# Key products with both token parts in one 512-column matmul, and an earlier first fetch of the gate grid

## The chip, the cores and the metric

One core of a Trainium2 chip runs the whole program. The metric is the device time of one execution in microseconds (us); lower is better. The engines are TensorE (PE; its weight loads are shown apart as PEld), VectorE (DVE), ScalarE (ACT), GpSimd (POOL) and SyncE (SP), whose queue issues nearly all of the transfers.

## The reference

Two transformer blocks over 256 tokens of width 1024, one after the other. Only the last part of the second matters here, a PEER layer: a retrieval among 128 x 128 = 16384 experts of one neuron each.

```
def peer(h, w_query, sub_keys, u_experts, v_experts):      # per chunk of 128 tokens
    qh = (xc @ w_query).reshape(128, 8, 256)
    s1, s2 = scores of the two halves of qh against 128 sub keys each
    v1, i1 = top_k(s1, 16);  v2, i2 = top_k(s2, 16)
    vs, ci = top_k(all 256 sums v1 + v2, 16)
    idx = e1 * 128 + e2                                    # the 16 experts of each head
    g = softmax(vs)
    z = einsum('td,thkd->thk', xc, u_experts[idx])         # key products
    a = gelu(z) * g
    return einsum('thk,thkd->td', a, v_experts[idx])       # value products
```

## The kernel before

Everything before the PEER layer is left alone by the change. The kernel computes the PEER layer densely: for all 16384 experts it forms the key products, and multiplies them by gates that are zero for the experts not chosen. Single precision is kept by splitting each operand into a rounded part `hi` and a rest `lo`, and summing three products, hi x hi, hi x lo and lo x hi (`mm3`, lines 118 to 122).

**Key stage.** 128 blocks of 128 experts (index `e2`) go through `up` (line 919). A block's weights (512 KB) are loaded by SP into a `raw` buffer (line 79, three buffers, loaded three blocks ahead), copied to `whi` by ScalarE (line 91) and subtracted to `wlo` by VectorE (line 92), two blocks ahead, three buffers each. Then 8 chunks of the depth, three matmuls each, 128 x 128 weights against 256 token columns, sum into one PSUM tile `pw` of the pool `psw` (two buffers): weights hi x tokens hi (line 120), hi x lo (line 121), lo x hi (line 122). ScalarE reads `pw` through the gelu into the tile `big` (line 928).

Beside these blocks the generator `select` (line 973) picks the experts of the 8 heads on VectorE, 1.25 steps for each block (`SEL_RATE`); every ninth block up to the 64th is preceded by two blocks of a head's query weights (`query`, line 954), which go through the same `mm3`. For each pair of heads it exponentiates on ScalarE (line 1030) and starts 32 indirect transfers on POOL (line 935), which add the gates of tokens 128 to 255 into a DRAM scratch `gscr`. When `select` is through, the gates of tokens 0 to 127 are made from one-hot matrices, 4 tokens at a time, in the remaining blocks: two one-hot tiles `o1` and `o2` on VectorE (line 1073, `GB` = 3 buffers each), a scaling on ScalarE (line 1076), four matmuls (line 1082), a multiplication into `big` for the blocks already there (line 1084, VectorE) and a copy for those to come (line 1086, ScalarE). A block that comes after some tokens' gates is then read in two parts: the tokens that are `done` through a small tile `gl` (lines 926, 927), the rest as before.

**Value stage.** For each pair of blocks, tokens 128 to 255 of `big` are multiplied by the gates fetched from `gscr` (`gated_pair`, lines 1122 and 1126; 256 KB fetched for each 4 blocks), `big` is split into `ah` and `al` (line 127), and for each block twelve matmuls of 512 columns (lines 356 to 358) add into four PSUM tiles `acc` of the pool `psa`. Its tiles lie in a pool `vs` that opens when the key stage's pool `gs` closes; `gf` and `fy` take the places of the token tiles `h2hi` and `h2lo`.

Instructions are put in an order on each engine by a planner that works with estimated durations; each engine then takes its own list strictly in that order. `issue_after(ins)` forces what is traced in the block behind `ins` on the same engine, without a wait.

Of the kernel before, what the change touches and what calls it, by code (L numbers as in the profile page):

```python
# [43 lines left out]
GB = 3  # L44
SB = 2
# [17 lines left out]
class Stream:  # L63
# [11 lines left out]
    def _load(self, i):  # L75
        ap = self.blocks[i]
        w = ap.shape[-1]
        r = self.pool.tile([P, self.width], F32, name="raw", tag="raw", bufs=self.raw_bufs)
        self.nc.sync.dma_start(out=r[:, :w], in_=ap)
        self.raw[i] = (r, w)  # L80

    def _split(self, i):
# [5 lines left out]
        with ExitStack() as es:  # L88
# [3 lines left out]
            self.nc.vector.tensor_sub(lo[:, :w], r[:, :w], hi[:, :w])  # L92
# [812 lines left out]
def peer(k, x, pool, hp, stream, u):  # L905
# [4 lines left out]
    with ExitStack() as es:  # L910
# [8 lines left out]
        def up(e2, done, gl):  # L919

            w = stream.next()
            ps = k.psw.tile([P, T], F32, name="pw", tag="w")
            end = wtype(k, w, 0, u, KC, ps)
            if done:
                g = gl.tile([P, P], F32, name="gl", tag="gl", bufs=2)
                nc.scalar.activation(g[:, :done], ps[:, :done], AF.Gelu_apprx_tanh)
                nc.vector.tensor_tensor(out=big[:, e2, :done], in0=g[:, :done], in1=big[:, e2, :done], op=ALU.mult)
            nc.scalar.activation(big[:, e2, done:], ps[:, done:], AF.Gelu_apprx_tanh)  # L928
# [17 lines left out]
        with k.tc.tile_pool(name="tk", bufs=1, reuse_waits="tile") as tk:  # L946
# [26 lines left out]
            def select():  # L973
                for h in range(H):
# [48 lines left out]
                    if h % 2:  # L1023
# [5 lines left out]
                                                op=ALU.subtract)  # L1029
                        nc.scalar.activation(e, e, AF.Exp)  # L1030
                        den = k.small.tile([P, 2, NT], F32, name="den", tag="den")
# [32 lines left out]
        with k.tc.tile_pool(name="gs", bufs=1, reuse_waits="tile") as gs:  # L1064
# [22 lines left out]

            done = made = 0
            start = e2
            ready = []  # L1090
            while e2 < P:
# [12 lines left out]
        with k.tc.tile_pool(name="vs", bufs=1, reuse_waits="tile") as gs:  # L1104
            gf = hp.tile([P, 2, D], F32, name="gf", tag="h2hi")
            ada_rows(k, gf[:, 0, :], 5)
            nc.sync.dma_start(out=gf[:, 1, :], in_=a["final_g"].to_broadcast([P, D]))
            fy = hp.tile([P, NT, D], F32, name="fy", tag="h2lo")
# [8 lines left out]
            grids = {}  # L1117

            def gated_pair(e0):
                if e0 % GQ == 0:  # L1120
                    g = grids[e0 // GQ] = gs.tile([P, GQ, P], F32, name="gt", tag="gt", bufs=2)
                    ins = nc.sync.dma_start(out=g, in_=grid[:, e0:e0 + GQ, :]).ins
                    for p in added:
                        k.tc.add_manual_dep(ins, p.name, order, reason="all heads have added their gates")
                b = big[:, e0:e0 + 2, P:]
                nc.vector.tensor_tensor(out=b, in0=b, in1=grids[e0 // GQ][:, e0 % GQ:e0 % GQ + 2, :], op=ALU.mult)  # L1126

            def parts(e0):
                ah = gs.tile([P, 2, T], F32R, name="ah", tag="ah", bufs=SB)
# [243 lines left out]
```

## Time and profile before

| | |
|---|---|
| three runs | 1714.48, 1718.57, 1720.56 us; median 1718.57 |
| profiled execution | 1715.93 us, its span 1714.2 us |
| mean granted TensorE clock | 0.991 of 2.4 GHz |
| busy over the span | PE 97%, PEld 89%, DVE 73%, ACT 50%, POOL 19% |
| key stage (from about 884 to 1342 us of the span) | 458 us |
| value stage (from about 1350 to 1702 us) | 352 us |

Busy time of an engine is the time in which at least one of its instructions runs. The span runs from the first to the last instruction; the execution is 1.7 us longer. A matmul's duration in the trace is longer than the time between two starts, because matmuls are pipelined; so rates are read from starts.

### The profile page before, as it was taken

Reading aid. Unit: us, or ns where it says so; the run is one execution under the profiler, and the core shown is the slowest. Engines: PE = TensorE matmul, PEld = TensorE weight load, DVE = VectorE, ACT = ScalarE, POOL = GpSimd, SP = SyncE. Lnnn points to the kernel's source line nnn. Section 1 sums busy time; section 2 is a strip of 40 time slices with the busy share of each in tenths; the row PEclk is TensorE's granted clock in tenths of the full one; section 3 lists DMA queues with packets and bytes.
Section 4 is the critical chain, followed back from the end, with each engine's and each line's share of the span. In section 5 each row is a group of like instructions: output and inputs, shape, how many; then the busy total and the mean of one; then the engine's idle time right before and its main releaser. Section 6 shows DMA issues by size and latency. Waiting matters only on the chain.

```text
span 1714.2 us, 28850 instructions
## 1 busy us (share of the span) xinstructions
PE 1670.0 (97%) x11106; PEld 1529.4 (89%) x11106; DVE 1252.1 (73%) x2081; ACT 864.2 (50%) x1399; POOL 318.5 (19%) x227
## 2 busy tenths in 40 slices
PE   8999999999999999999999999999999799999997
PEld 7899899888999999878889999999999688888886
DVE  6867789776867878865768878877777577555555
ACT  6554444336544544354544454457666344444443
POOL 1000000000000000036200787877700000000000
PEclk9999999999999999999999999999999899999999
DMA  8567678976456668966135777776655687666664
GB/s 312 181 196 217 202 248 289 360 237 208 136 160 185 225 183 294 339 215 205 60 118 182 176 186 172 173 173 149 156 153 160 209 281 238 193 195 187 195 188 131
DMA packets 115721, 345.70 MB, mean 202 GB/s; under 512 B 29856, under 2 KB 31104, under 8 KB 114688
## 3 DMA queue, kind: packets, MB, share of 16 engines
q1 hardware_dynamic: 95104, 336.23, 61.0%
q0 software_dynamic: 20480, 7.63, 4.2%
q8 instruction: 87, 1.43, 0.3%
q14 instruction: 50, 0.41, 0.1%
HBM read 342.66 MB, written 11.64 MB: 207 GB/s over the span
## 4 chain that ended last, share of the span: by engine, by line
PE 74%; issue 11%; DVE 8%; DMA 5%; ACT 2%; POOL 1%; SPq 0%; POOLq 0%; DVEq 0%; ACTq 0%
PE pw L122 13%; PE pw L121 13%; PE pw L120 13%; PE acc L358 10%; PE acc L357 10%; PE acc L356 10%; DMA gt<-gscr 3%; DVE wlo L92 2%; PE pst L1082 2%; PE po L476 1%; ACT whi L91 1%; PE pst L174 1%; DVE i L888 0%; PE pst L468 0%; DVE big L1126 0%
## 5 line engine op out<-in xcount | busy, mean ns | idle before, releaser
L91 ACT ACTIVATE whi<-raw 128x1024 fp32r<-128x1024 f32 (+1 forms) x549 | 573.3, 1048 | 593.6 <-PE pw L121 274.1
L92 DVE TENSOR_TENSOR wlo<-raw,whi 128x1024 fp32r<-128x1024 f32 (+1 forms) x549 | 667.2, 1220 | 252.3 <-ACT whi L91 246.2
L120 PE MATMUL pw<-h2hi,whi 128*128 128x256 f32 x1152 | 331.2, 287 | 0.9 <-ACT big L928 0.9
L122 PE MATMUL pw<-h2hi,wlo 128*128 128x256 f32 x1152 | 327.6, 284 | 1.8 <-DVE wlo L92 1.8
L121 PE MATMUL pw<-h2lo,whi 128*128 128x256 f32 x1152 | 327.3, 284 | 0.1
L120 PE MATMUL pw<-uhi,whi 128*128 128x256 f32 x1000 | 285.1, 285 | 0.0
L121 PE MATMUL pw<-ulo,whi 128*128 128x256 f32 x1000 | 284.4, 284 | 0.0
L122 PE MATMUL pw<-uhi,wlo 128*128 128x256 f32 x1000 | 284.4, 284 | 0.0
L935 POOL DMA_INDIRECT gscr<-gate,place x128 | 241.1, 1883 | 127.0 <-DVE first L1036 66.6
L122 PEld LDWEIGHTS pw<-h2hi,wlo 128*128 128x128 f32 x1152 | 222.2, 193 | 2.6 <-DVE wlo L92 2.6
L120 PEld LDWEIGHTS pw<-h2hi,whi 128*128 128x128 f32 x1152 | 222.4, 193 | 2.0 <-ACT big L928 1.7
L121 PEld LDWEIGHTS pw<-h2lo,whi 128*128 128x128 f32 x1152 | 222.4, 193 | 0.4 <-DVE h2lo L181 0.4
L356 PE MATMUL acc<-whi,ah 128*128 128x512 f32 x512 | 200.4, 391 | 8.1 <-ACT ah L127 8.1
L358 PE MATMUL acc<-whi,al 128*128 128x512 f32 x512 | 202.3, 395 | 0.4 <-DVE al L127 0.4
L357 PE MATMUL acc<-wlo,ah 128*128 128x512 f32 x512 | 201.4, 393 | 0.1
L121 PEld LDWEIGHTS pw<-ulo,whi 128*128 128x128 f32 x1000 | 192.5, 193 | 1.3 <-issue 1.3
L120 PEld LDWEIGHTS pw<-uhi,whi 128*128 128x128 f32 x1000 | 192.5, 192 | 0.9 <-issue 0.7
L122 PEld LDWEIGHTS pw<-uhi,wlo 128*128 128x128 f32 x1000 | 192.5, 193 | 0.7 <-issue 0.7
L356 PEld LDWEIGHTS acc<-whi,ah 128*128 128x128 f32 x512 | 96.7, 189 | 29.6 <-ACT ah L127 8.3
L357 PEld LDWEIGHTS acc<-wlo,ah 128*128 128x128 f32 x512 | 96.7, 189 | 23.0 <-DVE wlo L92 0.5
L358 PEld LDWEIGHTS acc<-whi,al 128*128 128x128 f32 x512 | 96.7, 189 | 20.9 <-DVE al L127 1.2
L356 PE MATMUL acc<-whi,hhi 128*128 128x512 f32 x256 | 99.9, 390 | 0.0
(257 smaller groups left out, 2411.0 us busy)
## 6 DMA issues: line engine op xcount, KB each, us to landing
raw<-in_w_layers_dram SPq DMA_DIRECT2D x240, 512.0 KB
raw<-in_u_dram SPq DMA_DIRECT2D x128, 512.0 KB
raw<-in_v_dram SPq DMA_DIRECT2D x128, 512.0 KB
aw<-in_w_ada_dram SPq DMA_DIRECT2D x48, 512.0 KB
gscr<-in_zeros_dram SPq DMA_DIRECT2D x16, 512.0 KB
raw<-in_w_query_dram SPq DMA_DIRECT2D x16, 512.0 KB
gt<-gscr SPq DMA_DIRECT2D x32, 256.0 KB
raw<-in_w_qkb_dram SPq DMA_DIRECT2D x8, 512.0 KB
```

The costliest lines, as they stand in the source:

```text
L91: self.nc.scalar.activation(hi[:, :w], r[:, :w], AF.Copy)
L92: self.nc.vector.tensor_sub(lo[:, :w], r[:, :w], hi[:, :w])
L120: nc.tensor.matmul(out, a[0], b[0], start=first, stop=False)
L121: nc.tensor.matmul(out, a[0], b[1], start=False, stop=False)
L122: return nc.tensor.matmul(out, a[1], b[0], start=False, stop=last).ins
L174: k.nc.tensor.transpose(ps[:, c, :], src[:, (c0 + c) * P:(c0 + c + 1) * P], k.ident)
L356: nc.tensor.matmul(acc, a[0], w[0][:, o:o + cols], start=first, stop=False)
L357: nc.tensor.matmul(acc, a[0], w[1][:, o:o + cols], start=False, stop=False)
L358: return nc.tensor.matmul(acc, a[1], w[0][:, o:o + cols], start=False, stop=last).ins
L476: nc.tensor.matmul(po[:, h, :], pT[:, i, :], v[:, c, vcol(h):vcol(h) + DH], start=(c == 0), stop=(c == nchunk - 1))
L935: ins = nc.gpsimd.indirect_dma_start(out=k.gscr, out_offset=bass.IndirectOffsetOnAxis(ap=place[:, h, j:j + 1], axis=0), in_=gate[:, h, j:j ...
L1082: nc.tensor.matmul(ps[:, i, :], o1[:, i, :], o2[:, i, :], start=True, stop=True)
```

## The change

It does four things. (1) The tokens' two parts lie beside each other in one tile `both`, and each chunk of a key block takes one matmul of 512 columns, weights hi x (tokens hi, tokens lo), and one of 256, weights lo x tokens hi. The two halves of the sum now lie in two halves of a PSUM tile of the pool `psa` (four buffers), and `total` joins them: ScalarE copies the second half, VectorE adds the first, ScalarE takes the gelu in place. Query blocks stay as they were. (2) The value stage's tiles share the key stage's pool, with `ah` and `al` in the places of `o1` and `o2` (two buffers each, one fewer than before), and its beginning moves into the key loop: the first fetch of the gates after the weight load issued last at block 120, the first two multiplications after the load and split issued last at block 125, and the first split before block 127. Each later fetch is issued one group of four blocks earlier. (3) `gf` and `fy` become parts of one tile in the place of `both`. (4) `select` pauses before and after its exponential, so that a pair of heads takes 23 steps instead of 21.

```
-GB = 3
-SB = 2
+GB = 2
+FETCH = 8
+AHEAD = 3
...
-        self.nc.sync.dma_start(out=r[:, :w], in_=ap)
+        self.last_load = self.nc.sync.dma_start(out=r[:, :w], in_=ap).ins
...
-            self.nc.vector.tensor_sub(lo[:, :w], r[:, :w], hi[:, :w])
+            self.last_split = self.nc.vector.tensor_sub(lo[:, :w], r[:, :w], hi[:, :w]).ins
...
-            ps = k.psw.tile([P, T], F32, name="pw", tag="w")
-            end = wtype(k, w, 0, u, KC, ps)
+            ps = k.psa.tile([P, 2, T], F32, name="pw", tag="acc")
+            for c in range(KC):
+                o = slice(c * P, (c + 1) * P)
+                nc.tensor.matmul(ps.rearrange("p i t -> p (i t)"), w[0][:, o], both[:, c].rearrange("p i t -> p (i t)"),
+                                 start=c == 0, stop=False)
+                end = nc.tensor.matmul(ps[:, 0, :], w[1][:, o], u[0][:, c, :], start=False, stop=c == KC - 1).ins
+
+            def total(out, part):
+                nc.scalar.activation(out, ps[:, 1, part], AF.Copy)
+                nc.vector.tensor_tensor(out=out, in0=ps[:, 0, part], in1=out, op=ALU.add)
+                nc.scalar.activation(out, out, AF.Gelu_apprx_tanh)
+
             if done:
                 g = gl.tile([P, P], F32, name="gl", tag="gl", bufs=2)
-                nc.scalar.activation(g[:, :done], ps[:, :done], AF.Gelu_apprx_tanh)
+                total(g[:, :done], slice(0, done))
                 nc.vector.tensor_tensor(out=big[:, e2, :done], in0=g[:, :done], in1=big[:, e2, :done], op=ALU.mult)
-            nc.scalar.activation(big[:, e2, done:], ps[:, done:], AF.Gelu_apprx_tanh)
+            total(big[:, e2, done:], slice(done, T))
...
+                        yield
                         nc.scalar.activation(e, e, AF.Exp)
+                        yield
...
+            def fetch(e0):
+                g = gs.tile([P, GQ, P], F32, name="gt", tag="gt", bufs=2)
+                ins = nc.sync.dma_start(out=g, in_=grid[:, e0:e0 + GQ, :]).ins
...
+            def gated_pair(e0):
+                if e0 % GQ == 0 and e0 + GQ < P:
+                    fetch(e0 + GQ)
+                b = big[:, e0:e0 + 2, P:]
+                nc.vector.tensor_tensor(out=b, in0=b, in1=grids[e0], op=ALU.mult)
...
+                if e2 == P - FETCH:
+                    with k.tc.issue_after(stream.last_load):
+                        fetch(0)
+                if e2 == P - AHEAD:
+                    with k.tc.issue_after(stream.last_load), k.tc.issue_after(stream.last_split):
+                        gated_pair(0)
+                        gated_pair(2)
+                if e2 == P - 1:
+                    split_pairs = [parts(0)]
+
+            rows = hp.tile([P, 2 + NT, D], F32, name="rows", tag="h2")
+            gf, fy = rows[:, 0:2, :], rows[:, 2:, :]
...
-            u = [hp.tile([P, KC, T], F32R, name=n) for n in ("h2hi", "h2lo")]
+            both = hp.tile([P, KC, 2, T], F32R, name="h2", tag="h2")
+            u = [both[:, :, 0, :], both[:, :, 1, :]]
```

## Rows read from the trace of the kernel before

**Rows 1.** The page, busy time of each engine over the whole span.
```profile
PE 1670.0 (97%) x11106; PEld 1529.4 (89%) x11106; DVE 1252.1 (73%) x2081; ACT 864.2 (50%) x1399; POOL 318.5 (19%) x227
```
**Rows 2.** Busy time by stretch: PE, PEld, DVE, ACT, POOL, granted clock, DMA share, GB/s.
```profile
884.00:1148.00 264.00, 261.26 (x2166) 259.63 (x2166) 219.16 (x636) 132.34 (x203) 162.01 (x86) 1.00 0.70 177
1148.00:1342.00 194.00, 192.16 (x1605) 191.75 (x1604) 146.46 (x206) 127.08 (x327) 79.06 (x43) 0.99 0.60 156
1342.00:1350.00 8.00, 0.06 (x1) 0.06 (x1) 2.19 (x4) 1.84 (x5) 0.61 (x1) 0.70 0.94 321
1350.00:1362.00 12.00, 11.55 (x40) 8.86 (x41) 7.80 (x15) 3.62 (x5) 0.00 (x0) 0.78 0.54 159
```
**Rows 3.** PE's timeline between the stages: start, duration, line, tile, [idle before].
```profile
1341.52 0.28 PE L122 MATMUL pw<-h2hi,wlo 128*128 128x256 f32 x1
1349.94 0.80 PE L356 MATMUL acc<-whi,ah 128*128 128x512 f32 x1 [8.15 <-ACT ah L127]
...
1355.50 0.39 PE L358 MATMUL acc<-whi,al 128*128 128x512 f32 x1
```
**Rows 4.** The SP queue's timeline in the same stretch.
```profile
1341.83 0.33 SPq L1107 DMA_DIRECT2D gf<-in_final_g_dram  x1
1342.47 0.82 SPq L1122 DMA_DIRECT2D gt<-gscr  x2
```
**Rows 5.** VectorE's timeline in the same stretch.
```profile
1348.80 0.76 DVE L1126 TENSOR_TENSOR big<-big,gt 128x256 f32<-128x256 f32 x2 [4.57 <-DMA gt<-gscr]
```
**Rows 6.** PE's timeline in a key block: first and last of eight matmuls.
```profile
1333.12 0.28 PE L121 MATMUL pw<-h2lo,whi 128*128 128x256 f32 x1
...
1333.96 0.28 PE L122 MATMUL pw<-h2hi,wlo 128*128 128x256 f32 x1
```
**Rows 7.** PE's timeline in a value block: first and last of ten matmuls.
```profile
1495.81 0.39 PE L357 MATMUL acc<-wlo,ah 128*128 128x512 f32 x1
...
1497.87 0.39 PE L357 MATMUL acc<-wlo,ah 128*128 128x512 f32 x1
```
**Rows 8.** VectorE's groups by shape: count, busy us, mean ns, idle before.
```profile
L92 DVE TENSOR_TENSOR wlo<-raw,whi 128x1024 fp32r<-128x1024 f32 x533 | 652.5, 1229 | 235.4 <-ACT whi L91 229.4 <-PE pw L122 3.1 <-issue 0.9
...
L603 DVE TENSOR_TENSOR xp<-pw,cc 128x256 f32<-128x256 f32 x8 | 3.4, 424 | 0.3
...
L927 DVE TENSOR_TENSOR big<-gl,big 128x128 f32<-128x128 f32 x3 | 0.9, 284 | 0.0
```
**Rows 9.** ScalarE's groups by shape.
```profile
L91 ACT ACTIVATE whi<-raw 128x1024 fp32r<-128x1024 f32 x533 | 561.6, 1057 | 572.2 <-PE pw L121 270.6 <-PE acc L358 206.1 <-issue 47.4
...
L969 ACT ACTIVATE s<-sk 128x256 f32<-128x256 f32 x16 | 5.2, 382 | 0.0
```
**Rows 10.** Two neighbouring stretches of 14 us in the selection, columns as in group 2.
```profile
912.00:926.00 14.00, 14.00 (x120) 14.00 (x119) 9.60 (x15) 7.20 (x12) 0.00 (x0) 1.00 0.69 212
926.00:940.00 14.00, 14.00 (x119) 14.00 (x119) 13.97 (x56) 6.60 (x9) 0.00 (x0) 1.00 0.54 170
```
**Rows 11.** PE's waits in the key stage: us in total, times, longest.
```profile
PE pw L122 <- DVE wlo L92: 1.8, 4, 0.5
...
PE pw L120 <- ACT big L928: 0.9, 4, 0.2
```
**Rows 12.** VectorE's longest wait during selection, 884 to 1148 us.
```profile
DVE wlo L92 <- ACT whi L91: 38.1, 25, 2.0
```
**Rows 13.** VectorE's two longest waits in the rest of the key stage, 1148 to 1342 us.
```profile
DVE o L1073 <- PE pst L1082: 27.6, 24, 1.5
...
DVE wlo L92 <- ACT whi L91: 15.3, 21, 2.0
```
**Rows 14.** ScalarE's timeline around one of the four exponentials.
```profile
1070.40 1.28 ACT L1030 ACT_TABLE_LOAD   x1
1073.12 0.26 ACT L1030 ACTIVATE ex<-ex 128x64 f32<-128x64 f32 x1 [1.44 <-DVE ex L1028]
```
**Rows 15.** POOL's gate transfers: duration min/median/max, first and last start.
```profile
L935 POOL DMA_INDIRECT gscr<-gate,place x128: 1542/1698/3197, 944.7 to 1244.0; - x128
```

More of the change, by code (lines that the diff above doesn't have):

```diff
@@ L902, in peer_stream, with peer @@
     return Stream(k.tc, pool, blocks, D, 3, 3, 3, 2)
-def peer(k, x, pool, hp, stream, u):
+def peer(k, x, pool, hp, stream, u, both):
     nc = k.nc
@@ L1086, in gates, with parts @@
                     nc.scalar.activation(b[:, :, cur:], ps[:, :, cur:], AF.Copy)
+            grids = {}
+            def fetch(e0):
+                g = gs.tile([P, GQ, P], F32, name="gt", tag="gt", bufs=2)
+                ins = nc.sync.dma_start(out=g, in_=grid[:, e0:e0 + GQ, :]).ins
+                for p in added:
+                    k.tc.add_manual_dep(ins, p.name, order, reason="all heads have added their gates")
+                for i in range(0, GQ, 2):
+                    grids[e0 + i] = g[:, i:i + 2, :]
+            def gated_pair(e0):
[3 more added lines that the diff above has]
+                nc.vector.tensor_tensor(out=b, in0=b, in1=grids[e0], op=ALU.mult)
+            def parts(e0):
+                ah = gs.tile([P, 2, T], F32R, name="ah", tag="o1", bufs=GB)
+                al = gs.tile([P, 2, T], F32R, name="al", tag="o2", bufs=GB)
+                split(nc, ah, al, big[:, e0:e0 + 2, :])
+                return ah, al
             done = made = 0
@@ L1102, in peer @@
                         done = t0 + 4
-        with k.tc.tile_pool(name="vs", bufs=1, reuse_waits="tile") as gs:
-            gf = hp.tile([P, 2, D], F32, name="gf", tag="h2hi")
+                if e2 == P - FETCH:
[9 more added lines that the diff above has]
+            gf, fy = rows[:, 0:2, :], rows[:, 2:, :]
             ada_rows(k, gf[:, 0, :], 5)
             nc.sync.dma_start(out=gf[:, 1, :], in_=a["final_g"].to_broadcast([P, D]))
-            fy = hp.tile([P, NT, D], F32, name="fy", tag="h2lo")
             acc = [[k.psa.tile([P, 512], F32, name="acc", tag="acc") for _ in range(2)] for _ in range(NT)]
@@ L1115, in value @@
                 return tok_mm(nc, acc[t][h], (sh[:, c], sl[:, c]), w, h * 512, 512, e == 0, e == P - 1)
[L1117 to L1129, printed above, removed]
-                al = gs.tile([P, 2, T], F32R, name="al", tag="al", bufs=SB)
-                split(nc, ah, al, big[:, e0:e0 + 2, :])
-                return ah, al
-            gated_pair(0)
-            gated_pair(2)
-            split_pairs = [parts(0)]
             for e0 in range(0, P, 2):
@@ L1157, in peer @@
             ss = [k.small.tile([P, 2], F32, name="ss", tag="ss") for _ in range(NT)]
-            xg = gs.tile([P, 512], F32, name="xg", tag="ah", bufs=SB)
+            xg = gs.tile([P, 512], F32, name="xg", tag="o1", bufs=GB)
             r = {}
@@ L1253, in body @@
             stream.after = norm_cols(k, x, *norm, *u)
-        peer(k, x, pool, hp, stream, u)
+        peer(k, x, pool, hp, stream, u, both)
 def _pack_t(w, c):
```

## The prediction

> **What bounds the kernel now.** I read the page first. TensorE is busy for 1670.0 of 1714.2 us, VectorE for 1252.1 [rows 1], so a gain must come either from less TensorE time or from the few places where TensorE stands. The busy time by stretch shows where the change lies: the key stage, whose two parts of 264 and 194 us together leave TensorE idle for 4.6 us (2.74 + 1.84), and the 8 us behind it in which it does nothing [rows 2]. VectorE is the second engine of the key stage: 219.16 + 146.46 = 365.6 us of 458, 80%; ScalarE has 259.4, 57% [rows 2].
>
> The gap between the stages is read on three timelines. TensorE's last key matmul starts at 1341.52, its first value matmul at 1349.94, after 8.15 us of waiting for `ah` [rows 3]. What is late is the gates: SP issues the first two fetches only at 1342.47, behind `gf`, which cannot be written before the last key matmul has read its place [rows 4], and VectorE's first multiplication starts at 1348.80 [rows 5]. The pause costs more than itself. The granted clock falls to 0.70 and 0.78 in these stretches [rows 2], and the 11 value matmuls that start from 1349.94 on take until 1355.50, 5.56 us [rows 3], where at the later pace (2.06 us for nine intervals, 0.2289 each [rows 7]) they would take 2.52. So the boundary costs 8.15 + 3.04, about 11.2 us.
>
> **The matmuls.** Key matmuls of 256 columns start every 0.120 us (seven intervals in 0.84 [rows 6]); a block of 24 takes 2.88. After the change a chunk has one of 512 columns and one of 256. No row shows the two in turn. The best the 512 could do is 256 more columns at one a cycle of 2.4 GHz (the 0.1089 between the two rates of [rows 6, 7] comes near it), 0.1067 on top of 0.120, together 0.2267, a gain of 0.0133 a chunk; the worst is no gain over two starts of 0.120. I take the value stage's 0.2289, the same width, operand types and weight load [rows 7]: 0.2400 - 0.2289 = 0.0111 a chunk, 0.089 a block, and for 128 x 8 chunks **-11.4 us** (bounds 0 and -13.6). The change takes a third of the key matmuls away and hardly any of their columns; only what a matmul costs beyond its columns is saved.
>
> The rows show 0.120 - 0.1067 = 13 ns beyond the columns at 256 and 0.2289 - 0.2133 = 16 ns at 512. The Trainium skill (TensorE: Matmul & The Clock Gate, Part 1, on the gap of 56 ns) puts this fixed part at about 2.5 ns for a warm matmul. By it the estimate would be 2.5 ns x 1024 = 2.6 us in place of the 11.4; this trace shows a larger part, and the trace decides.
>
> **The boundary.** The first fetch moves from behind the key stage to block 120, 8 blocks of 2.79 us or 22 us before its end. POOL's last transfer of gates starts at 1244.0, some 75 us earlier [rows 15], so the fetch waits for nothing; in the queue it stands between weight loads, and half of the 22 us covers more than the 6.3 us from issue to first use of before [rows 4, 5]. The multiplications (two in 0.76 [rows 5]) and the first split get the last three blocks, 8.4 us, where no one-hots are left. What is late next: the fourth accumulator needs the bank of the last key block, whose copies and additions take some 2 us beside a `whi` of 1.06 [rows 9], but it is first written nine matmuls, 2.06 us, into the stage. `gf` still holds SP's queue until the key stage ends, as before [rows 4]; three blocks of value weights are loaded ahead by then, which covers 8.2 us (36 matmuls of 0.2289). So **-11.2 us**, bounds -11.5 and 0.
>
> **The pauses at the exponential.** TensorE's idle waits in the key stage are 1.8 us for `wlo` and 0.9 for `pw`'s bank, four each [rows 11], as many as there are exponentials. There ScalarE loads a table at 1070.40, then waits 1.44 us for the subtraction [rows 14]. The pauses let the subtraction pass first, and four banks replace two: **-2 us** (bounds 0 and -2.7). They also lengthen the selection: 84 steps, 5 spent waiting for scores and 2 at the end fill 73 blocks at 1.25 a block; eight more steps make 76, which leaves 52 instead of 55 blocks for the one-hots. The 32 groups of four tokens fit in either.
>
> **The crowding of VectorE.** `total` adds, for each block, a ScalarE copy (0.382 for 256 columns [rows 9]) and a VectorE addition out of PSUM (0.424 [rows 8]); from the one-hots on, two of each at half the width, near 0.284 each on VectorE [rows 8]. That is 128 x 0.424 = 54 us and 52 x (2 x 0.284 - 0.424) = 7.5 us, 62 in all; instructions on VectorE overlap, two of 0.42 ran in 0.76 [rows 5], 0.08 for each, and 180 of these make 14, so 48 at least. I take 54. VectorE then needs 365.6 + 54 = 420 us of a key stage of 458 - 11.4 - 2 = 445: 94%. ScalarE needs 259.4 + 55 or 314, 71%, and is not the bound.
>
> VectorE was full for stretches already: 13.97 of 14 us, between stretches of 9.60 in which it waits for the next scores [rows 10], and TensorE stood in neither. In a full stretch it now gets 0.34 to 0.42 us more a block while the block gets 0.09 shorter, so it falls behind by about 0.47. A full stretch is some 22 us, 7.6 blocks: 3.6 us behind. Splits run two blocks ahead, 5.6 us, of which `whi` and `wlo` take 1.06 + 1.23 [rows 8, 9]: 3.3 us of cover. So each of eight heads may lose some 0.3 to 1 us: 6 us. In the one-hot part VectorE needs 146.5 - 4 (three blocks fewer) + 24, or 166 of 181 us, with one buffer fewer; its 27.6 us of waiting for a buffer [rows 13] is mostly an engine that came early, and can be used. I put 3 us there. Together **+9 us**; bounds 0, where all idle time can be used, and about 25, where a tenth of the stage stays idle for VectorE (420 / 0.9 = 467 against 445).
>
> **Sum.** 1715.9 - 11.4 - 11.2 - 2 + 9 = 1700.3 us against the profiled execution. This one lies 2.6 us under the median of the runs, so the forecast for a median is **1703 us**; I give it as 1702.5, with 1695 to 1711 as its own range.
>
> **Rivals.** A measurement of this kernel can tell a change of 0.3%, 5.2 us, from none: faster means under 1713.4, slower over 1723.7, on the median's level.
>
> (1) VectorE's waits stay. They are 38.1 us for `whi` during selection, 27.6 for a one-hot buffer and 15.3 for `whi` after [rows 12, 13], 81 in all, and each stands in VectorE's list in front of other work. If a part w of them stays in place when additions come in between, the key stage takes 420 + w. With w = 49 (60%) the key stage has grown by 11, and the kernel is where it was; from w = 55 (67%) it is slower, and with all 81 it takes 1718.6 + 43 - 11 = 1750 us. For it speaks that each addition waits for a ScalarE copy and so adds waits of its own; against it, that these waits are early arrivals, which lateness eats first. Slower: 8%. A middle case, w about 40 to 55, gives 1710 to 1723: 14%.
>
> (2) The 512-column matmul costs two of 256, as it would if the excess went with the columns or with a weight load that no longer hides. Then 11.4 us are missing, the crowding is milder (+6): 1711. Equal weight loads and types in [rows 6, 7] speak against it: 7%. The part of 2.5 ns on the skill's page (above) would put the kernel near this rival, at 1702.5 + 8.8 - 2 = 1709.
>
> [...] 13%.
>
> The forecast keeps 58%. Rival 2 and most of rival 3 still end faster: 58 + 6 + 10 and a third of the middle case, 4, make 0.78 faster; the rest of the middle case and of (2) and (3) 0.14 the same; 0.08 slower. The range, from all terms at their best (1715.9 - 13.6 - 11.5 - 2.7 + 2.6 = 1690.7, hardly reached) to the middle case's upper part, is 1693 to 1718.
>
> **What the next profile would show.** A key block without one-hots takes 2.79 us, matmuls starting 0.229 and 0.120 apart; were it 2.88, rival 2 holds. The value stage's first matmul starts within 1 us of the last key matmul, at a granted clock of 1.00; the fetch starts some 20 us before. VectorE is busy for 90 to 96% of the key stage and TensorE's waits for `wlo` add up to under 12 us there; over 25 us, or VectorE below 90% with TensorE waiting, is rival 1. The prediction is wrong if TensorE waits for one-hots or `wlo` longer than the boundary gives back.

## The result, and the profile after

The changed kernel takes 1694.39 us (median of 6 runs, 1690.12 to 1698.38) against 1717.27 (median of 6, 1714.48 to 1721.8): a ratio of 0.9873, interval 0.9854 to 0.9891, or 22.9 us less. The profiled execution is the quickest of its six, 1690.12 us with a span of 1688.3; the one of before has 1714.2. The two spans differ by 25.9 us, and that is the sum which the rows below account for.

The page, busy time of each engine over the whole span; [rows 1] are its partner:

```profile
PE 1653.2 (98%) x10082; PEld 1468.1 (87%) x10082; DVE 1296.1 (77%) x2257; ACT 906.3 (54%) x1575; POOL 299.1 (18%) x227
```

TensorE has 1024 matmuls fewer, as it should, and is busy for 16.8 us less; VectorE has 44.0 us more. Busy time by stretch of the changed kernel, columns as in [rows 2]:

```profile
876.00:890.00 14.00, 10.75 (x77) 9.44 (x76) 10.56 (x15) 7.55 (x12) 0.99 (x1) 1.00 0.35 112
...
884.00:1148.00 264.00, 263.60 (x1650) 236.06 (x1649) 244.64 (x715) 162.59 (x287) 157.03 (x91) 1.00 0.73 186
1148.00:1322.00 174.00, 173.12 (x1081) 154.30 (x1080) 161.41 (x302) 135.89 (x410) 64.43 (x38) 1.00 0.63 162
1322.00:1334.00 12.00, 10.30 (x45) 7.50 (x44) 9.79 (x22) 7.73 (x18) 0.60 (x1) 1.00 0.90 312
1334.00:1402.00 68.00, 67.13 (x293) 54.70 (x292) 52.50 (x84) 32.16 (x36) 0.00 (x0) 1.00 0.84 275
1402.00:1672.00 270.00, 270.00 (x1180) 221.29 (x1179) 156.46 (x152) 130.56 (x148) 0.00 (x0) 1.00 0.63 192
```

In the key stage VectorE is now busy for 244.64 + 161.41 = 406 of 438 us, 93%, and TensorE stands for 0.40 + 0.88 = 1.3 us, where it stood for 4.6 [rows 2]. The engine that is almost full costs nothing there. The place in which TensorE still stands is new: 1.70 us in the 12 us around the start of the value stage and 0.87 in the 68 behind them; from 1402 on it never stands. PE's timeline at the boundary, as in [rows 3]:

```profile
1317.83 0.40 PE L926 MATMUL pw<-h,whi 128*128 128x512 f32 x1
...
1323.13 0.40 PE L926 MATMUL pw<-h,whi 128*128 128x512 f32 x1
1323.37 0.28 PE L928 MATMUL pw<-h,wlo 128*128 128x256 f32 x1
1323.49 0.39 PE L357 MATMUL acc<-whi,ah 128*128 128x512 f32 x1
...
1326.89 0.47 PE L357 MATMUL acc<-whi,ah 128*128 128x512 f32 x1 [1.39 <-DVE big L932]
```

The first value matmul starts 0.12 us after the last key matmul; the pause of 8.15 us [rows 3] is gone, and the granted clock, 0.70 and 0.78 in the two stretches of before [rows 2], stays at 1.00. A wait for a PSUM bank (the piece of PSUM that one tile takes) comes in its place. The matmul at 1326.89, the seventh of the value stage, is the first into the third accumulator. That accumulator takes the bank of the last key block but one, whose addition VectorE starts only at 1326.47, 5.9 us after the block's last matmul; TensorE stands for 1.39 us, and later 0.30 us for the last block's bank under the fourth accumulator. Why the first split is in time is read on the SP queue, as in [rows 4]:

```profile
1292.56 0.33 SPq L1105 DMA_DIRECT2D gt<-gscr  x1
1295.21 13.87 SPq L80 DMA_DIRECT2D raw<-in_u_dram  x5
1309.13 0.42 SPq L1105 DMA_DIRECT2D gt<-gscr  x1
...
1320.05 2.38 SPq L1105 DMA_DIRECT2D gt<-gscr  x2
1323.24 3.46 SPq L80 DMA_DIRECT2D raw<-in_v_dram  x2
```

The first fetch is issued 31 us before the key stage ends, 50 us earlier in the span than before. The fetches do not stop there, though: nothing holds the later ones and their multiplications back, so they run on between the loads of the value weights; the last of the 32 is issued at 1401.1, 278 us before the last value matmul. ScalarE's and TensorE's waits from 1323 to 1420 us, each by its engine (us in total, times, longest):

```profile
ACT whi L92 <- DMA raw<-in_v_dram: 16.9, 12, 3.1
...
PE acc L357 <- DVE big L932: 1.7, 2, 1.4
PE acc L358 <- DVE wlo L93: 0.9, 1, 0.9
```

The first line is value weights that land late, the second the banks, the third a split that comes late. Counted from one matmul's start to the next, beyond the usual 0.229, the two waits for banks cost 2.2 us and the late `wlo` 1.4. Fetches that run ahead are not new, though. The kernel before issues its 32 within 86 us as well, and its ScalarE waits as long for value weights (fetches: count, duration min/median/max in ns, first and last issue; waits from 1350 to 1435 us):

```profile
L1122 SPq DMA_DIRECT2D gt<-gscr x32: 319/327/864, 1342.5 to 1428.7; - x32
...
ACT whi L91 <- DMA raw<-in_v_dram: 18.2, 10, 3.2
```

There no wait of TensorE for `wlo` is listed. That its pause of 8 us had given the loads and splits a start is the likely reason, but no run tests it.

VectorE's waits in the key stage, the first line from 884 to 1148 us, the two others from 1148 to 1322; [rows 12, 13] are their partners:

```profile
DVE wlo L93 <- ACT whi L92: 16.7, 14, 1.7
...
DVE wlo L93 <- ACT whi L92: 0.7, 1, 0.7
...
DVE o L1086 <- PE pst L1095: 0.4, 1, 0.4
```

The 81 us of waits of before have become 17.8, and VectorE's idle time in the key stage fell from 92 us (458 - 366 [rows 2]) to 32. The additions took the time in which VectorE had been early.

**Where the 25.9 us lie.** From the first key matmul to the last the kernel before takes 460.6 us (880.9 to 1341.5), the changed one 442.4 (880.9 to 1323.4): 18.2 us less. From there to the first value matmul it is 8.4 against 0.1: 8.3 less. From the first value matmul to the last it is 354.8 against 355.5, 0.6 more, though the 354.8 held the 3.0 us of low clock; so 3.7 us are given back in that stage. The last matmul stands 9.4 us before the end of the span in both. Of the 18.2, about 10.4 are the matmuls' pace: the 592 pairs of neighbouring chunks from 884 to 1148 us start 0.349 us apart on the mean, where 660 of 691 triples of before start 0.36 apart, and behind them 381 pairs take 0.357 where 386 triples take 0.366 (both include a first matmul after a transposition, some 0.08 longer, about 30 times). That is 0.011 x 620 + 0.009 x 400. Another 3.3 are TensorE's shorter waits. The rest, some 4.5, is a remainder, and part of it goes with the granted clock: in the profile of before it is 0.76 from 876 to 890 us and 0.90 from 1148 to 1165, in that of after 1.00 in both (0.76 and 0.90 are means of the full 2.4 GHz and half of it). In the first stretch the first 24 key matmuls, the same in both kernels, take 4.63 against 3.46 us, 1.2 more. In the second, 0.90 over 17 us misses 1.7 us of the full clock, an estimate of the loss. The other 1.6 stay unexplained. Those two dips come and go between executions (kernels below whose first stages are equal show 0.76 and 1.00 alike), and no run tests what makes them; the medians, which differ by 3.0 us less than the spans, are the better measure.

### The profile page after: what moved, and what is told of

Its sections match the earlier page's. It is cut to its first block, busy times and chain, and to the rows that moved or that the text cites. A ratio compares the mean times of both kernels' runs of the same rounds, so it can differ in the third digit from the quotient of the medians.

```text
span 1688.3 us, 27147 instructions
## 1 busy us (share of the span) xinstructions
PE 1653.2 (98%) x10082; PEld 1468.1 (87%) x10082; DVE 1296.1 (77%) x2257; ACT 906.3 (54%) x1575; POOL 299.1 (18%) x227
## 4 chain that ended last, share of the span: by engine, by line
PE 79%; DVE 11%; DMA 4%; ACT 2%; issue 2%; POOL 1%; SPq 0%; POOLq 0%; DVEq 0%; ACTq 0%
PE acc L358 12%; PE acc L357 12%; PE acc L359 12%; PE pw L123 9%; PE pw L121 9%; PE pw L122 9%; PE pw L926 8%; PE pw L928 4%; DVE wlo L93 4%; DMA gt<-gscr 3%; PE pst L1095 1%; PE po L477 1%; ACT whi L92 1%; DVE big L932 1%; DVE big L1097 1%
## 5 line engine op out<-in xcount | busy, mean ns | idle before, releaser
L926 PE MATMUL pw<-h,whi 128*128 128x512 f32 x1024 | 362.9, 398 | 0.0
L928 PE MATMUL pw<-h,wlo 128*128 128x256 f32 x1024 | 285.6, 279 | 0.0
L946 POOL DMA_INDIRECT gscr<-gate,place x128 | 221.5, 1730 | 130.2 <-DVE first L1049 67.2
L926 PEld LDWEIGHTS pw<-h,whi 128*128 128x128 f32 x1024 | 192.3, 188 | 43.0
L359 PE MATMUL acc<-whi,al 128*128 128x512 f32 x512 | 198.7, 388 | 0.0
L928 PEld LDWEIGHTS pw<-h,wlo 128*128 128x128 f32 x1024 | 192.9, 188 | 0.2 <-DVE wlo L93 0.2
L358 PE MATMUL acc<-wlo,hhi 128*128 128x512 f32 x256 | 99.8, 390 | 0.0
L359 PE MATMUL acc<-whi,hlo 128*128 128x512 f32 x256 | 99.6, 389 | 0.0
```

What stands on the lines that cost most here:

```text
L358: nc.tensor.matmul(acc, a[0], w[1][:, o:o + cols], start=False, stop=False)
L359: return nc.tensor.matmul(acc, a[1], w[0][:, o:o + cols], start=False, stop=last).ins
L926: nc.tensor.matmul(ps.rearrange("p i t -> p (i t)"), w[0][:, o], both[:, c].rearrange("p i t -> p (i t)"), start=c == 0, stop=False)
L928: end = nc.tensor.matmul(ps[:, 0, :], w[1][:, o], u[0][:, c, :], start=False, stop=c == KC - 1).ins
L946: ins = nc.gpsimd.indirect_dma_start(out=k.gscr, out_offset=bass.IndirectOffsetOnAxis(ap=place[:, h, j:j + 1], axis=0), in_=gate[:, h, j:j ...
```

## The experiments

Each has its own ratio to the kernel before on the same chip. In the table the stages are those of the profiled execution: key stage from first to last matmul start, pause from there to the first value matmul, value stage from its first to its last matmul start; "key" names the matmuls (old: three of 256 columns).

| kernel | key | median us | ratio and interval | key stage | pause | value stage |
|---|---|---|---|---|---|---|
| before | old | 1717.27 | | 460.6 | 8.4 | 354.8 |
| after | new | 1694.39 | 0.9873 (0.9854 to 0.9891) | 442.4 | 0.1 | 355.5 |
| x_again | new | 1693.43 | 0.9872 (0.9857 to 0.9888) | 443.3 | 0.1 | 355.8 |
| x_boundary | old | 1711.26 | 0.9968 (0.9956 to 0.998) | 459.0 | 0.1 | 356.5 |
| x_matmul | new | 1704.13 | 0.9931 (0.9918 to 0.9944) | 443.0 | 13.9 | 356.4 |
| x_nopause | new | 1692.49 | 0.9873 (0.9856 to 0.9889) | 441.2 | 0.2 | 359.1 |
| x_noadd | new | 1694.14 | 0.9873 (0.9853 to 0.9893) | 442.2 | 0.1 | 356.0 |
| x_add2 | new | 1708.81 | 0.9961 (0.9946 to 0.9976) | 457.3 | 1.6 | 356.8 |
| x_late | new | 1764.85 | 1.0287 (1.0274 to 1.03) | 517.0 | 2.6 | 351.8 |
| x_unbound | new | 1754.19 | 1.023 (1.0209 to 1.0251) | 503.8 | 0.1 | 355.6 |
| x_paced | new | 1690.11 | 0.9852 (0.9834 to 0.987) | 446.6 | 0.1 | 352.6 |
| x_bpaced | old | 1702.87 | 0.9925 (0.9912 to 0.9939) | 458.2 | 0.1 | 351.3 |
| x_best | new | 1689.91 | 0.9854 (0.9839 to 0.987) | 443.7 | 0.1 | 351.4 |
| x_best_group | new | 1689.11 | 0.9841 (0.9828 to 0.9855) | 443.6 | 0.1 | 358.2 |

**x_boundary: the changed kernel with the old matmuls.** The fetch, the first multiplications, the shared pool and the pauses stay; a key block is three matmuls of 256 columns a chunk again, into two banks, and the gelu reads PSUM.

```
-            ps = k.psa.tile([P, 2, T], F32, name="pw", tag="acc")
...
+            ps = k.psw.tile([P, T], F32, name="pw", tag="w")
+            end = wtype(k, w, 0, u, KC, ps)
```

> The key blocks go back to three matmuls of 256 columns and a gelu straight from PSUM; the shared pool, the early fetch and the pauses stay. Theory (the parts add up: boundary about 9 us, matmul rate about 11, pauses and their clock about 3): 1717 - 12 = 1705 us, ratio to before 0.993, the first value matmul within 1 us of the last key matmul. Rival A (crowding eats the matmuls' gain, all of the 23 us come from boundary and pauses): 1694 to 1697 us, ratio 0.988. Rival B (the boundary needs what the new matmuls bring): 1712 or more.

Measured: 1711.26 us over 12 runs, 5.3 us faster than before, not the 11.2 that the boundary had been given. The gap is closed, though, and TensorE itself never waits for the gates. Its PE line at the boundary; then its fetches (columns as above), and the waits of ScalarE, VectorE and TensorE from 1344 to 1420 us:

```profile
1343.83 0.28 PE L123 MATMUL pw<-h,wlo 128*128 128x256 f32 x1
1343.95 0.39 PE L357 MATMUL acc<-whi,ah 128*128 128x512 f32 x1
...
L1095 SPq DMA_DIRECT2D gt<-gscr x32: 320/327/891, 1311.7 to 1421.0; - x32
...
ACT whi L92 <- DMA raw<-in_v_dram: 31.4, 19, 3.7
DVE big L1105 <- DMA gt<-gscr: 19.4, 17, 5.0
...
PE acc L358 <- DVE wlo L93: 3.3, 3, 2.0
```

All 32 fetches (256 KB each) go out within 109 us, among the loads of the weights that the value stage needs now. ScalarE waits 31.4 us for these weights, and VectorE, in whose list multiplications stand in front of splits, 19.4 us for gates. TensorE then waits for `wlo`, which needs both. The value stage takes 356.5 us, 4.7 more than the 351.8 of before without its slow start (354.8 - 3.0). So the gap goes and part of it returns as late splits; x_bpaced below tests that, though not which of the two makes them late.

**x_matmul: the kernel before with the new matmuls alone.** `both`, the pair of matmuls and `total` are put in; the fetch stays at the boundary, the value stage in its own pool, three buffers, no pauses.

```
-            ps = k.psw.tile([P, T], F32, name="pw", tag="w")
-            end = wtype(k, w, 0, u, KC, ps)
+            ps = k.psa.tile([P, 2, T], F32, name="pw", tag="acc")
...
+                nc.tensor.matmul(ps.rearrange("p i t -> p (i t)"), w[0][:, o], both[:, c].rearrange("p i t -> p (i t)"),
```

> The kernel before with the new key matmuls, the copy and addition, and nothing else of the change (no pauses, the value stage begins after the key stage, three one-hot buffers). Theory: 1717 - 11 = 1706 us, ratio 0.9935, a gap of about 8 us between the stages with the clock low behind it, a key block of about 2.80 us. Rival A: 1714 to 1718 us, since VectorE's extra 54 us cost what the matmuls give; TensorE's waits for wlo and one-hots then add up to 8 us or more in the key stage.

Measured: 1704.13 us, 12.4 faster than before, as the theory had it. But the key stage gives 17.7 us in the profile and the pause grows. PE at the boundary, the SP queue and VectorE's first multiplications (x3):

```profile
1341.59 0.79 PE L356 MATMUL acc<-whi,ah 128*128 128x512 f32 x1 [13.57 <-ACT ah L127]
...
1331.02 0.38 SPq L1118 DMA_DIRECT2D rows<-in_final_g_dram  x1
...
1340.44 1.10 DVE L1136 TENSOR_TENSOR big<-big,gt 128x256 f32<-128x256 f32 x3 [7.27 <-DMA gt<-gscr]
```

The last key matmul starts at 1327.73. Before, SP passed `gf` 0.3 us after the last key matmul (1341.83 against 1341.52 [rows 3, 4]); here it does so 3.3 us after, since VectorE, fuller now, ends its splits later and SP's loads wait for their buffers (the split from 1329.34 to 1330.57 holds the last load in front of `gf`). The multiplication follows 9.4 us behind `gf` instead of 7.0 [rows 4, 5]. So 5.4 us of what the matmuls save fall into the pause, and the boundary part removes those too: 12.4 + 5.3 for the parts alone and 5.4 for this make 23.1, against 22.9 for both. The 5.4 comes from one execution, the slowest of its five (1709.14 us), and each of the other three numbers has an interval of 2 to 3 us to either side, so the close agreement is partly luck.

**x_nopause: the changed kernel without the two pauses at the exponential.**

```
-                        yield
                         nc.scalar.activation(e, e, AF.Exp)
-                        yield
```

> The changed kernel without the two pauses of select. Theory: TensorE waits some 0.5 to 1 us at each of the four exponentials, 2 to 3 us in all: 1697 us, ratio to before 0.988 to 0.989. Rival C (with VectorE 93% busy the stall of ScalarE can no longer be made up): 1 to 2 us at each and 4 to 8 in all, 1699 to 1702. Rival D: the pauses do nothing, 1694.

Measured: 1692.49 us, the same ratio as the changed kernel, 0.9873. All of TensorE's waits from 881 to 1323 us:

```profile
PE pst L1055 <- DVE first L1027: 0.6, 1, 0.6
PE pw L122 <- DVE h L182: 0.3, 1, 0.3
```

No wait for `wlo` or a bank of `pw` is left at the exponentials, without any pause. The converse stands in x_boundary, which has the pauses but the old matmuls with their two banks: there both waits of [rows 11] remain (881 to 1327 us):

```profile
PE pw L123 <- DVE wlo L93: 1.9, 4, 0.5
PE pw L121 <- ACT big L929: 1.0, 4, 0.3
```

So the 2.7 us are removed by the new matmuls and their four banks, which no run separates, and the pauses do nothing that the median shows. (The value stage of this one profile is 3.6 us longer, by waits for `wlo`; the medians do not repeat that.)

**x_late: the fetch back behind the key stage, in the shared pool.** It asks whether the position of the work or the shared pool closes the gap.

```
-                if e2 == P - FETCH:
-                    with k.tc.issue_after(stream.last_load):
-                        fetch(0)
...
             nc.sync.dma_start(out=gf[:, 1, :], in_=a["final_g"].to_broadcast([P, D]))
+            fetch(0)
+            gated_pair(0)
+            gated_pair(2)
+            split_pairs = [parts(0)]
```

> The changed kernel with the first fetch, the first multiplications and the first split behind the key loop and behind gf, in the shared pool. Theory (what counts is when the fetch is issued): the gap of about 8 us and the low clock come back, less the waits of about 2 us that the changed kernel has at its first value blocks: 1694 + 8 = 1702 us, ratio 0.991. Rival E (the pool's opening was what held the fetch; sharing it is enough, since the planner issues the fetch early by itself): 1694 to 1697.

Measured: 1764.85 us, 2.9% slower than before; both theories missed. With the pool shared, the tile's place is free long before, and the planner, which orders the instructions of a queue, puts the unbound fetch far ahead of `gf`. SP's wait and TensorE's, from 1140 to 1420 us:

```profile
SPq L1105 <- DMA gscr<-gate,place: 68.5, 1, 68.5
...
PE pw L926 <- DVE gl L932: 62.6, 1, 62.6
```

The queue stands for 68.5 us on a fetch that has to wait for POOL's last gates, with the weight loads behind it. VectorE stands as well, 66.9 us in front of the first multiplication by the gates, which is unbound too, and TensorE waits 62.6 us for an addition behind that. So the experiment says nothing of a late fetch, but a good deal of the binding, which x_unbound tests by itself.

**x_unbound: the changed kernel without the binding of the first fetch.**

```
-                    with k.tc.issue_after(stream.last_load):
-                        fetch(0)
+                    fetch(0)
```

> The changed kernel with the first fetch issued at block 120 of the program, but not bound behind the weight load. Theory (the planner, which takes POOL's gate transfers for shorter than they are, moves a fetch that hangs on nothing else ahead in SP's list; SP then stands until the last gate is added, and the weights behind it): a hole of some 60 us in the key stage while POOL ends, 1750 to 1765 us, ratio 1.02 to 1.03. Rival I (the place at block 120 is enough): 1694, ratio 0.987.

Measured: 1754.19 us, 60 more than the changed kernel and 37.7 more than before. The SP queue, and the waits of SP and TensorE from 1140 to 1420 us:

```profile
1154.33 7.82 SPq L80 DMA_DIRECT2D raw<-in_u_dram  x3
1230.40 0.33 SPq L1105 DMA_DIRECT2D gt<-gscr  x1
...
SPq L1105 <- DMA gscr<-gate,place: 68.0, 1, 68.0
...
PE pst L1095 <- ACT gl L933: 58.6, 1, 58.6
```

Between two loads of key weights the queue stands for 68 us, until the gates are added. That the fetch is written at block 120 does not place it there; the binding does.

**x_noadd: the changed kernel without the copy and the addition of `total`.** The gelu reads the first half of PSUM, so that the product of the weights' high part with the tokens' low part is left out of the result; the matmuls stay.

```
-                nc.scalar.activation(out, ps[:, 1, part], AF.Copy)
-                nc.vector.tensor_tensor(out=out, in0=ps[:, 0, part], in1=out, op=ALU.add)
-                nc.scalar.activation(out, out, AF.Gelu_apprx_tanh)
+                nc.scalar.activation(out, ps[:, 0, part], AF.Gelu_apprx_tanh)
```

> The changed kernel without the copy and the addition: the gelu reads the first half of the sum, so the product of weights hi and tokens lo is left out of the result, while the matmuls stay. This is the price of total by itself. Theory (VectorE and ScalarE are hidden in the key stage; only the waits of 2.6 us at the first value blocks go): 1691 to 1694 us, ratio 0.986. Rival H (the crowding costs what the prediction put, 9 us): 1684 to 1686, ratio 0.981.

Measured: 1694.14 us, 0.9873 again. Busy time by stretch, and TensorE's longest wait from 884 to 1350 us:

```profile
884.00:1148.00 264.00, 263.86 (x1649) 237.28 (x1648) 223.93 (x642) 140.02 (x213) 156.19 (x80) 0.99 0.72 184
1148.00:1322.00 174.00, 173.31 (x1085) 154.76 (x1084) 140.29 (x201) 119.94 (x311) 84.08 (x49) 1.00 0.64 162
...
PE acc L358 <- DVE wlo L93: 1.6, 2, 1.0
```

VectorE loses 406 - 364 = 42 us of work in these 438, and the kernel gains nothing. Even at the boundary, where the bank's wait goes, a wait for `wlo` stands instead. The price of joining the two halves is nil, within the 5 us or so that the two intervals leave open. The two key stages, 442.2 and 442.4 us, say a little less than they seem to: this profile has the clock dip at 876 to 890 us (0.76; the first 24 key matmuls take 5.18 us, against 3.46), so up to 1.7 us may hide there.

**x_add2: the changed kernel with one more VectorE instruction behind each addition,** a maximum of the tile with itself, which changes no value: 128 x 0.41, about 52 us.

```
                 nc.vector.tensor_tensor(out=out, in0=ps[:, 0, part], in1=out, op=ALU.add)
+                nc.vector.tensor_tensor(out=out, in0=out, in1=out, op=ALU.max)
```

> The changed kernel with one more VectorE operation behind each addition of total (a maximum of the sum with itself, which leaves the values as they are). It brings VectorE some 128 x 0.36 + 51 x 0.12 or 52 us more in the key stage, where it is busy for 406 of 438. Theory (VectorE's idle time can nearly all be used, and behind that it is the bound): 458 us of work in 438, the key stage grows by 20 to 30 us: 1714 to 1724, ratio to before 0.998 to 1.004; TensorE waits for wlo or one-hots by as much. Rival F (the waits that are left on VectorE are fixed, so that each microsecond added to it is added to the end): 52 us, 1746. Rival G (hidden): 1694 to 1698.

Measured: 1708.81 us, 14.4 more than the changed kernel, under the theory's 20 to 30. Busy time by stretch, and TensorE's longest wait from 884 to 1322 us:

```profile
884.00:1148.00 264.00, 258.77 (x1606) 231.35 (x1607) 255.49 (x761) 159.11 (x273) 149.94 (x79) 0.99 0.69 177
1148.00:1322.00 174.00, 170.05 (x1042) 149.37 (x1041) 172.23 (x386) 136.10 (x388) 95.06 (x50) 1.00 0.62 154
...
PE pw L928 <- DVE wlo L93: 5.5, 8, 1.4
```

Now VectorE is busy for 427.7 of 438 us, 98%, TensorE stands for 9.2 in them, and the stage is 14.9 us longer, some 1.8 of which are the clock dip at its start (the first 24 key matmuls take 5.22 us). Of the 52 us added some 37 still went into idle time. So the crowding that the prediction feared exists, but sets in above the load of the changed kernel.

**x_paced: the later fetches bound to the loads and splits of the value stage.** Each fetch stands behind the weight load issued last in SP's list, and each multiplication behind the split issued last in VectorE's, so that the gates go out at the pace at which they are used.

```
                 if e0 + 4 < P:
-                    gated_pair(e0 + 4)
+                    with k.tc.issue_after(stream.last_load), k.tc.issue_after(stream.last_split):
+                        gated_pair(e0 + 4)
```

> The changed kernel with every multiplication by the gates and every fetch bound behind the weights' last load and split, so that they keep step with the value blocks instead of being done by 1401 us. Theory (256 KB fetches that run ahead make the first value weights late, 16.9 us of ScalarE's waits for them and 0.9 to 2 us of TensorE's): TensorE's waits for wlo in the first 80 us of the value stage go, 1692 us, ratio 0.986. Rival J (hidden there): 1694.

Measured: 1690.11 us. The ratio, 0.9852, lies under that of the changed kernel, but the intervals overlap. The mechanism shows in the profile: the fetches, and TensorE's only wait from 1329 to 1420 us:

```profile
L1105 SPq DMA_DIRECT2D gt<-gscr x32: 327/424/431, 1298.5 to 1644.6; - x32
...
PE acc L357 <- DVE big L932: 0.7, 2, 0.5
```

The fetches reach to 1644.6 instead of 1401.1, ScalarE no longer waits for value weights, TensorE's waits for banks fall from 1.7 to 0.7 us and those for `wlo` go, and the stage takes 352.6 us instead of 355.5. At the 0.2289 us of [rows 7] from start to start its 1536 matmuls take 351.4.

**x_bpaced: the same pacing on x_boundary,** where more had been lost.

```
                 if e0 + 4 < P:
-                    gated_pair(e0 + 4)
+                    with k.tc.issue_after(stream.last_load), k.tc.issue_after(stream.last_split):
+                        gated_pair(e0 + 4)
```

> The boundary part alone (old key matmuls), with multiplications and fetches kept in step with the value blocks. The boundary part by itself gave 1711.3 us, 5 us where 11 had been put, and its value stage waited 3.3 us for wlo and ran longer by that. Theory (fetches that run ahead, no longer behind a pause of 8 us, make value weights late and take back a part of the gap): those waits go, 1707 to 1708 us, ratio to before 0.995, and the value stage lasts some 353 us from its first matmul to its last. Rival K (the shortfall is elsewhere, in the key stage): 1711, ratio 0.997.

Measured: 1702.87 us, better than expected: 12.6 under the kernel before, where x_boundary had 5.3 (two chips, each against its own runs of before). The waits of `whi` for its data fall from 31.4 to 2.0 us, VectorE's for gates from 19.4 to none, TensorE waits for nothing from 1340 to 1420 us, and the value stage takes 351.3 us instead of 356.5. That is 5.2 of the 7.3 us. The other 2.1 are not explained by the pacing: in the profiles the first key matmul starts at 882.5 us instead of 884.8, in a part that no edit touches, and the granted clock from 876 to 890 us is 1.00 here and 0.76 there.

**x_again: the changed kernel once more,** beside x_bpaced, x_best and x_best_group on their chip.

```
 (no edit)
```

> The changed kernel once more, on the chip of the next three: 1694 us, ratio to before 0.987, in its earlier interval of 0.9854 to 0.9891.

Measured: 1693.43 us, 0.9872; the result repeats.

**x_best: the changed kernel, paced, with the last two key blocks' sums in the other PSUM pool,** so that no value accumulator waits for a bank.

```
-            ps = k.psa.tile([P, 2, T], F32, name="pw", tag="acc")
+            pool, tag = (k.psw, "w") if e2 >= P - 2 else (k.psa, "acc")
+            ps = pool.tile([P, 2, T], F32, name="pw", tag=tag)
...
```

> The changed kernel with fetches and multiplications kept in step with the value blocks and with the last two key blocks' sums in the other PSUM pool, so that the value stage's accumulators need not wait for them. Theory: 2.9 us from the pacing and up to 1.7 from the bank: 1689 to 1691 us, ratio to before 0.984 to 0.985; no wait for the last sums at the first value blocks. Rival: the bank's wait was beside another, and nothing is gained over 1690.

Measured: 1689.91 us (four runs, 1687.51 to 1691.65), 3.5 under x_again on the same chip (four runs, 1691.0 to 1693.88) and 25.5 under the kernel before; its interval, 0.9839 to 0.987, lies just under the changed kernel's median ratio and overlaps its interval. Busy time by stretch after the boundary:

```profile
1322.00:1344.00 22.00, 22.00 (x102) 18.18 (x101) 16.96 (x28) 13.39 (x26) 0.61 (x1) 1.00 0.79 266
1344.00:1402.00 58.00, 58.00 (x255) 47.58 (x254) 36.55 (x43) 27.60 (x32) 0.00 (x0) 1.00 0.71 221
```

TensorE does not stand for a moment where it stood for 2.6 us. The bank by itself is worth no more than the runs can tell (x_paced has the same median); with the pacing this version and the next have the lowest medians of all, clear of the kernel before and at the edge of what can be told from the changed kernel.

**x_best_group: x_best with a block's eight wide matmuls first and its eight narrow ones behind them,** to see whether a change of width costs anything.

```
             for c in range(KC):
...
                 nc.tensor.matmul(ps.rearrange("p i t -> p (i t)"), w[0][:, o], both[:, c].rearrange("p i t -> p (i t)"),
                                  start=c == 0, stop=False)
+            for c in range(KC):
+                o = slice(c * P, (c + 1) * P)
                 end = nc.tensor.matmul(ps[:, 0, :], w[1][:, o], u[0][:, c, :], start=False, stop=c == KC - 1).ins
```

> As the version before it, with a block's eight matmuls of 512 columns first and its eight of 256 behind. Theory (the rate is set by columns and a fixed part of each matmul, in whatever order): a block of 2.79 us as in the changed kernel, whose pairs take 0.347 to 0.353, and the same time within 2 us. Rival L (the change between widths costs some 4 ns a pair): 2.77 us or less a block, 4 us faster, 1685 to 1686.

Measured: 1689.11 us (1685.67 to 1695.6), the same as x_best. The order of the widths costs nothing that can be told.

## Why the prediction was right, and where its steps were not

The forecast was 1702.5 us, with 1695 to 1711 as its own range and 1693 to 1718 over all; measured are 1694.4, 0.6 below the first and inside the second. The direction held; the kernel is 8 us better than the forecast. The crowding, +9, did not come, and the boundary gave 3.7 less than said: that the sum missed by no more than 8 is in part luck. Of what the next profile was to show, a key block of 2.79 us (8 x 0.349), a first value matmul within 1 us, a clock of 1.00, VectorE at 90 to 96% and waits for `wlo` under 12 us all came; the fetch started 31 us before the end, not 20.

**The matmuls, -11.4: right.** The pace gives about 10.4 us (above), near the value taken from the value stage's rows. The 2.5 ns a matmul of the Trainium skill (TensorE: Matmul & The Clock Gate, Part 1, on the gap of 56 ns) would have given 2.6 us, an estimate; each of the 1024 matmuls taken away saved some 10 ns, and the measurement decides. Rival 2, a matmul of 512 columns that costs two of 256, falls: a pair would start every 0.36 us, and it starts every 0.349. That x_matmul gains 12.4 us though its pause is 5.4 longer says that its key stage gives more than this term: TensorE's shorter waits are in it, and in its profile the better clock from 1148 to 1165 us. The pair without a pause on either side, x_bpaced and x_best on one chip, both paced, differs by 13.0 us.

**The boundary, -11.2: the gap closed as said, but the step took it for free.** Fetch, multiplications and split were in time and the clock stayed up, but 3.7 us come back in the value stage, in two waits that were given nothing. The larger, some 2.2 us, is the banks: the step gave an addition some 2 us, where VectorE's list, with splits and multiplications in it, brings the last block's but one 5.9 us after its matmuls, and it is the third accumulator that waits longest. The other, some 1.4 us, is late splits. The fetches behind the first run up to 278 us ahead of their use, beside the value weights; they did so before too, but behind a pause. With the old matmuls, whose sums lie in another pool than the accumulators, this second loss stands alone and is larger: the part gains 5.3 us (x_boundary), paced 12.6 (x_bpaced). Rival 3, a pause that stays, is wrong as a place: nothing stays between the stages, the loss lies behind them.

**The pauses, -2: right as a sum, wrong as a cause.** TensorE's idle time in the key stage went from 4.6 to 1.3 us, but x_nopause has it so without the pauses, and x_boundary keeps both waits with them. The new matmuls and their banks do it. The count of blocks does not follow from its terms, since 84 + 8 + 5 + 2 steps at 1.25 make 79 blocks and not 76; the profile has 51 blocks read in two parts against 54 before, three fewer, as was said.

**The crowding of VectorE, +9: the step that failed.** The load was right: 94% of the key stage said, 93% measured. The loss was not: "each of eight heads may lose some 0.3 to 1 us". TensorE waits 1.3 us in all, none of it for `wlo`, and x_noadd, which takes 42 us off VectorE, gains nothing. So this term is 0, its lower bound, as far as the runs can tell (the upper one, 467 against 445, is 22 and not 25). The estimate let a full stretch of 22 us fall behind by 0.47 us a block and gave it 3.3 us of cover; the profile shows that VectorE's waits, 81 us before, shrank to 17.8. They were early arrivals, and rival 1 with its middle case falls. x_add2 finds the edge: at 98% in the key stage TensorE stands for 9.2 us, and of 52 us more only some 15 are paid.

By what was measured the sum would have been -10.4 for the matmuls, -11.2 + 3.7 for the boundary, -3.3 for the waits and 0 for the crowding: -21.2, against -22.9 between the medians, whose interval is some 3 us to either side. What stays open is why the two dips of the clock come and go; they bear on the 2 us by which x_boundary is slower than its late splits explain.

## What to carry to other kernels

The in-order waits of a second engine are not a price in waiting: they are its slack as long as what it delivers is taken later, and taking a piece of work off that engine and adding as much again (x_noadd, x_add2) tells in two runs where the slack ends; here it ended between 93 and 98%. A transfer that is pulled forward in an in-order queue needs two things said of it: behind which load it may stand (without that, 68 us of a blocked queue) and at what pace those that follow it may run (without that, 5.2 us of late splits in x_boundary). And the parts of a change are not additive where one fills a gap that the other widens: run each alone before any of them is priced.

## What the runs showed that was not expected

The same matmuls run at two rates while the granted clock reads 1.00. From 1402 to 1670 us of the value stage, which is the same code in both, x_best and then x_best_group have (busy time by stretch, and the group of one line with its count, busy time and mean ns):

```profile
1402.00:1670.00 268.00, 268.00 (x1173) 219.92 (x1172) 169.02 (x195) 129.54 (x147) 0.00 (x0) 1.00 0.67 211
...
L359 PE MATMUL acc<-whi,al 128*128 128x512 f32 x391 | 153.3, 392 | 0.0
```

```profile
1402.00:1670.00 268.00, 268.00 (x1151) 217.06 (x1150) 166.22 (x192) 126.96 (x144) 0.00 (x0) 1.00 0.67 210
...
L359 PE MATMUL acc<-whi,al 128*128 128x512 f32 x384 | 152.6, 397 | 0.0
```

TensorE never stands in either, and yet one gets through 1173 matmuls and the other through 1151. From start to start over the whole stage that is 0.2289 and 0.2333 us each, 351.4 against 358.2 us, and the second is the slowest run of its kernel (1695.6). In all other profiles the middle of the value stage runs at 0.2289 or 0.2295 us. The changed kernel's own key stage has both rates in one execution: the pairs from 1317.83 to 1323.13 (above) start 5.30 / 15 = 0.353 us apart, those between the two rows below, from its PE timeline, 2.08 / 6 = 0.347.

```profile
1247.85 0.40 PE L926 MATMUL pw<-h,whi 128*128 128x512 f32 x1
...
1249.93 0.39 PE L926 MATMUL pw<-h,whi 128*128 128x512 f32 x1
```

Nothing in the rows tells what sets the rate. The 6.8 us between the two stages are most of the 8.1 between the two spans, so it can be a large part of what runs of one kernel differ by.
